# A two-layer hybrid decoder trunk on one core: two plain feed-forward blocks per layer in place of three, the second unit's head issued ahead of the first one's middle, and two token sums in one operation

## The chip, the cores and the metric

The kernel runs on one core of one Trainium2 chip. The metric is the device time of one execution in microseconds (us); the figure to compare is the median over several executions. Engines are called as the profile calls them: PE (TensorE, matmuls), PEld (its weight loads, which run beside its matmuls), DVE (VectorE), ACT (ScalarE), POOL (GpSimd) and SP (SyncE, which here only issues DMAs).

## The reference

Two decoder layers over 528 tokens (16 learned meta tokens and 512 real ones), model width 1024, in fp32. A layer is an attention part (a forgetting-attention head group and a retention head group behind one input projection, one output projection, residual) and a feed-forward part. Only the second is touched here:

```python
    hn = rmsnorm(h, ffn_norm_g)
    ff = jax.nn.silu(jnp.einsum('bld,df->blf', hn, w_gate)) * jnp.einsum('bld,df->blf', hn, w_up)
    return h + jnp.einsum('blf,fd->bld', ff, w_down)
```

w_gate and w_up are 1024 x 2816, w_down is 2816 x 1024. The meta tokens are dropped after the last norm, so the second layer's feed-forward part computes the 512 real tokens only.

## The kernel before, in words

**Layout.** Activations lie transposed: 128 features on the partitions, tokens along the free axis. The width of 1024 is `NK` = 8 tiles of 128, the 2816 hidden columns are `NF` = 22 blocks of 128, called f. Every product is done in three matmuls, because each fp32 operand is split into a high part (rounded to fp32r) and a low part (the rest): high x high, high x low, low x high. Each weight tile is split when it arrives, by one ACT copy (high part) and one subtraction (low part) on DVE, or on POOL in parts of the attention. In the feed-forward part POOL takes none of them.

**Plain blocks.** For f < `PLAIN` (3 before) gate and up are computed by `dense_steps`: 8 steps each, one per k, with six matmuls of 264 tokens in layer 0 and three of 512 tokens in layer 1. A job's step 1 and step 4 split the two halves of the next job's weights (`convert(j + 1, ...)`). `g_done` scales the gate sum and takes silu; `u_done` multiplies and splits the product into `ah` (ACT) and `al` (DVE), the input of the down projection (`acts[f]`).

**Units.** For f >= `PLAIN` gate and up of one f are computed together by a `Unit`: a scheme with seven half-size products in place of eight, on the two halves of the width (rows of the weights) and the two halves of the tokens. A half has w = 264 tokens in layer 0 and 256 in layer 1. One product is 4 k-steps of three matmuls of w tokens, so a unit has 7 x 12 = 84 matmuls. It needs sums of weights and sums of tokens:

- `head()`: two products, with the split gate weights (`make1`, job w1) and the plain tokens. It uses a bank x (pool `psa`) and a bank z (one half of a `psd` tile; the other half is y).
- `middle()`: three products, with job w2 (`make2`: two sums of gate and up weights, then a split) and the first half of job w3 (`make3`). It is the first to use the token sums `t`.
- `tail()`: two products, with the second half of w3 and job w4 (`make4`); its `done` adds the banks, takes silu, multiplies and splits into `ah`, `al`.

`need(j)` at the start of a product prepares job j and up to two unit or down jobs after it. `x_forms(k)`, k = 0..3, makes the token sums `t`: it scales two tiles of h into `S`, forms three differences there, and splits four pieces into `th` and `tl` (low part: one DVE operation of 4w elements a partition). `S` has two buffers, shared with the sums of weights.

**The order of the work.** PE executes the list `steps` as written (a manual schedule for PE alone). The other engines' instructions are ordered by a planner, which takes program order as the priority, takes what is ready in its own estimate of times, and lets blocks under `high_priority` go ahead. Each engine then executes its list strictly in that order. DMAs are issued from SP, in its own order. At the end of `ffn` further steps are put into the list: `squares` and `rstd` (the norm), the first gate's `g_done`, and the four `x_forms`, which are put 9 places apart, from place `NK + 4` on.

**Rounds.** `ROUNDS` groups the blocks f into (0, 3), (3, 7), (7, 11), (11, 15), (15, 19), (19, 22). While a round's units are computed, the down projection (`down_job`, `down`) of the round before is woven in: one pair of output tiles after each unit's middle and tail. In round 0 there is nothing to weave in. Jobs of units and down products (`add_job`) take turns between two rings of weight buffers, `whi`/`wlo` and `fwhi`/`fwlo`, of two buffers each; raw weights come into a ring of three buffers (`raw`) and one of two (`fraw`, w_up of the units). `psd` has two tiles of two banks, `psa` four banks.

The steps around the change, in the order in which PE meets them before: gate 0, up 0, gate 1, up 1, gate 2, up 2 (plain, `PLAIN` = 3), then unit 3: head, middle, down (first tile of the pair), tail, down (second tile), then unit 4, and so on.

Of the kernel before, what the change touches and what calls it, by code (L numbers as in the profile page):

```python
# [13 lines left out]
ALU = mybir.AluOpType  # L14

D = 1024
NK = D // 128
# [7 lines left out]
DFF = 2816  # L25
NF = DFF // 128
ROUNDS = ((0, 3), (3, 7), (7, 11), (11, 15), (15, 19), (19, 22))
PLAIN = 3
HB = NK // 2
EPS = 1e-6  # L30
NBLK = SEQ // 128
# [8 lines left out]
def hybrid_kernel(ctx, tc, x_t, w_in, w_fl, w_out, w_gate, w_up, w_down, vecs, b_fg, rope, decay, mask, ident, out_t):  # L40
    nc = tc.nc
# [95 lines left out]
    def vcol(c):  # L137
        return vec[:, c:c + 1]


    def split(hi, lo, src, pinned=False):
        pin(nc.scalar.copy(hi, src), pinned)
        pin(nc.vector.tensor_sub(lo, src, hi.bitcast(F32)), pinned)
# [53 lines left out]
    def dense_steps(src, parts, pool=False, banks=False, ahead=(1, 4), own=None, wait=None):  # L197

        j = len(jobs)
        jobs.append({"src": src, "pool": pool, "own": own})

        def chunk(k0, k, n, xs, cols, ps, done):
            def go():
                convert(j)
                if k == 0:
                    t = [psum_a() for _ in cols] if banks else psum()
                    ps.append(t)
                    ps.append(t if banks else [t[:, b] for b in range(2)])  # L210
                size = jobs[j]["w"][0][0]
                _, hi, lo = jobs[j]["w"][(k0 + k) // size]
                wk = (k0 + k) % size
                xh, xl = xs(k)
                for i, (w, x) in enumerate(((hi, xh), (hi, xl), (lo, xh))):
                    for b, (c0, c1) in enumerate(cols):
                        nc.tensor.matmul(ps[1][b][:, 0:c1 - c0], w[:, wk, :], x[:, c0:c1],  # L217
                                         start=(k == 0 and i == 0), stop=(k == n - 1 and i == 2))
                if k == n - 1:
                    done(ps[0]) if wait is None else wait.append(lambda: done(ps[0]))  # L220
                for half, at_step in enumerate(ahead):
                    if k0 + k == at_step:
                        convert(j + 1, 4 * half + 4)
            return go

        steps = []
        for k0, xs, n, cols, done in parts:
            ps = []
            steps += [chunk(k0, k, n, xs, cols, ps, done) for k in range(n)]
        return steps  # L230
# [42 lines left out]
    def fft(tag, dt=F32R, shape=(128, T), bufs=None):  # L273
        return phase["ffn"].tile(list(shape), dt, name=tag, tag=tag, bufs=bufs)
# [518 lines left out]
    def ffn(l, st, real, last):  # L793
        QC = REAL if real else FULL
        t0 = META if real else 0
        w = (T - t0) // 2
# [5 lines left out]
        def two(t):  # L802
            return t[:, t0:T].rearrange("p (a b) -> p a b", a=2)
# [4 lines left out]
        def g_done(f):  # L808
            def go(ps):
                sg = tt("sg")  # L810
                if isinstance(ps, list):
                    for v, (c0, c1) in zip(ps, QC):
                        nc.vector.scalar_tensor_tensor(sg[:, c0:c1], v[:, 0:c1 - c0], RSC, st["R"][:, c0:c1],
                                                       ALU.mult, ALU.mult)
                else:
                    nc.vector.scalar_tensor_tensor(sv(sg, real), pv(ps, real), RSC, sv(st["R"], real), ALU.mult, ALU.mult)
                silu(sv(sg, real))
                sgs[f] = sg
            return go

        def u_done(f):
            def go(ps):
                u = tt("tq")
                nc.vector.scalar_tensor_tensor(sv(u, real), pv(ps, real), RSC, sv(st["R"], real), ALU.mult, ALU.mult)
                nc.vector.tensor_mul(sv(u, real), sv(u, real), sv(sgs[f], real))
                fh, fl = act_tile(f)
                split(sv(fh, real), sv(fl, real), sv(u, real))
                acts[f] = (fh, fl)
            return go
# [4 lines left out]
        def x_forms(k):  # L834
            def go():
                if k == 0:
                    st["t"] = [[fft(f"t{p}{i}", shape=(128, 2, 4, w)) for p in "hl"] for i in range(2)]
                s = fft("S", F32, (128, 6, w), 2)
                a, b = ((h[k][:, c0:c1], h[HB + k][:, c0:c1]) for c0, c1 in HC)
                g0, g1 = vcol(V_FFN + l * NK + k), vcol(V_FFN + l * NK + HB + k)  # L840
                nc.scalar.activation(s[:, 0:2], two(h[k]), AF.Copy, scale=g0)
                nc.vector.tensor_sub(s[:, 2], s[:, 1], s[:, 0])
                for i in range(2):
                    nc.vector.scalar_tensor_tensor(s[:, 3 + i], b[1], g1, s[:, 1 + i], ALU.mult, ALU.subtract)
                nc.vector.scalar_tensor_tensor(s[:, 5], a[1], g1, s[:, 4], ALU.mult, ALU.subtract)
                th, tl = (t[:, k % 2] for t in st["t"][k // 2])
                split(th, tl, s[:, 2:6])
            return go
# [8 lines left out]
        def add_job(**job):  # L857
            job["ring"] = "f" if len(jobs) % 2 else ""
            jobs.append(job)
            return len(jobs) - 1  # L860
# [26 lines left out]
        class Unit:  # L887
            def __init__(self, f):
                self.f = f
                self.t = {}  # L890
                self.w1 = add_job(load=self.load, make=self.make1, n=NK)

            def rest(self):
# [91 lines left out]
        def down_job(p, f0, f1):  # L985

            n = f1 - f0
            t = {}

            def load():  # L990
                if t:
                    return
                t["r"] = wp.tile([128, NK, 128], F32, name="raw", tag="raw", bufs=3)
                for s in range(2):
                    nc.sync.dma_start(t["r"][:, s * n:s * n + n], w_down[l, 2 * p + s, :, f0:f1])

            return add_job(load=load, make=lambda hi, lo: splits(hi, lo, t["r"][:, 0:2 * n]), n=2 * n)
# [28 lines left out]
        steps = []  # L1026
        tails = []
        fills = []
        for r, (f0, f1) in enumerate(ROUNDS):
            for f in range(f0, f1):  # L1030
                if f < PLAIN:
                    steps += dense_steps(w_gate[l, f], [(0, xs, NK, QC, g_done(f) if f else held.append)], banks=f == 1)
                    steps += dense_steps(w_up[l, f], [(0, xs, NK, QC, u_done(f))])
                    continue
                u = Unit(f)
                steps += u.head()
                for v in tails:
                    v.last()
                    steps += v.tail()
                tails = []  # L1040
                u.rest()
                steps += u.middle()
                if fills:
                    p, g0, g1 = fills.pop(0)
                    j = down_job(p, g0, g1)
                    steps += down(j, 0, 2 * p, g0, g1, not real)
                    u.last()
                    steps += u.tail()
                    steps += down(j, 1, 2 * p + 1, g0, g1, False)
                else:  # L1050
                    tails = [u]
            for p, g0, g1 in fills:
                j = down_job(p, g0, g1)
                for s in range(2):
                    steps += down(j, s, 2 * p + s, g0, g1, False)
            fills = [(p, f0, f1) for p in range(NK // 2)]
# [157 lines left out]
                (after_0, after_1, after_2, after_3, after_4, after_5, after_6, after_7))]  # L1214
            steps += merge(rnd, places)
        for i in range(HB):
            steps.insert(NK + 4 + 9 * i, x_forms(i))
        steps.insert(NK + 4, lambda: g_done(0)(held[0]))
        steps.insert(NK + 4, lambda: rstd(st, QC))
        steps.insert(4, lambda: squares(st, QC, False, False))  # L1220
# [5 lines left out]
    def layer(l):  # L1226
# [79 lines left out]
        for g in range(2):  # L1306
# [15 lines left out]
                      ret_places(3, 52, 45.5, 47.5, 57.5, 55.5, 58.5, 60, 64.1, 63, 64.2))  # L1322
        plan += [op[3], op[7], op[11], op[15]] + op[16:]
        up = ffn(l, ff, real, real)
        plan += [lambda: enter("ffn"), start_ffn] + up
        return plan
# [78 lines left out]
```

## Time and profile before

| | before |
|---|---|
| time, median of 3 runs | 1272.0 us (1271.65 to 1273.03) |
| the profiled execution's own time | 1272.86 us |
| its span, first to last instruction | 1271.1 us |
| PE busy | 1256.1 us (99% of the span), 9271 matmuls |
| DVE busy | 996.9 us (78%), 1843 instructions |
| ACT busy | 687.2 us (54%) |
| POOL busy | 264.9 us (21%) |
| HBM traffic | 94 GB/s over the span |
| mean granted clock of PE | 0.997 |

Shares of busy time are averages over stages. The feed-forward part of layer 0 begins on PE at about 289.7 us (the first matmul that reads `xh`), that of layer 1 at about 913 us. In the rows of the profile a line shows the engine, the line of the kernel, the operation and "out<-in" by the tiles' names; L194, L217 and L191 are helpers that many steps share, and so are L868, L869 (the split of a unit's or down job's weights), L880 (a product of a unit), L142 and L143 (`split`). L1015 is a down projection's matmul, L914 to L927 the sums of weights, L841 to L845 the token sums. Matmul records overlap: a record of 264 tokens lasts some 0.28 us, while twelve of them follow one another in 1.45 us, so the time of PE is read from starts, or from the chain of work, and not from the sum of the records.

### The profile page before, as it was taken

The page shows a single profiled execution, that of the slowest core. Times are in us where ns is not written, and L with a number is a line of the kernel's source. Part 1 is how long each engine was busy: PE and PEld are TensorE (multiplying, and loading weights), DVE is VectorE, ACT ScalarE, POOL GpSimd, SP SyncE. Part 2 cuts the span into 40 slices and gives each one's busy share as a digit, 9 for nine tenths or more (in the row PEclk, how much of TensorE's full clock was granted, in tenths as well). Part 3 has the DMA queues.
Part 4 walks back from the last instruction along what each step waited for, and adds up shares of the span by engine and source line. Part 5 has one row for each costly group of instructions (what it writes and reads, how often), then busy time and mean ns, then how long its engine had stood idle before and what let it go on. Part 6 is the DMA issues. An engine that isn't in the chain of part 4 may idle for free.

```text
span 1271.1 us, 23615 instructions
## 1 busy us (share of the span) xinstructions
PE 1256.1 (99%) x9271; PEld 1197.9 (94%) x9271; DVE 996.9 (78%) x1843; ACT 687.2 (54%) x1246; POOL 264.9 (21%) x522
## 2 busy tenths in 40 slices
PE   9999999999999999999999999999999999999997
PEld 8999999999999999999999989999789999999996
DVE  7877856779988888887686877567899888888866
ACT  6666545676444444444455665457764444444444
POOL 3355546420000000000016546454100000000000
PEclk9999999999999999999999999999999999999998
DMA  6322222223333333332323132222233333333321
GB/s 217 93 68 84 78 90 76 73 71 113 108 96 100 100 100 101 100 100 84 101 76 116 61 101 85 76 92 68 100 95 121 100 100 100 101 100 100 103 80 67
DMA packets 45680, 120.57 MB, mean 95 GB/s; under 512 B 5360, under 2 KB 12272, under 8 KB 45568
## 3 DMA queue, kind: packets, MB, share of 16 engines
q1 hardware_dynamic: 45104, 118.74, 29.7%
q8 instruction: 73, 1.20, 0.4%
q10 hardware_dynamic: 464, 0.32, 0.1%
q14 instruction: 39, 0.32, 0.1%
HBM read 116.91 MB, written 2.13 MB: 94 GB/s over the span
## 4 chain that ended last, share of the span: by engine, by line
PE 92%; DVE 4%; ACT 2%; DMA 1%; issue 1%; ACTq 0%; DVEq 0%
PE psd L217 29%; PE psa L880 18%; PE psd L1015 14%; PE psd L880 13%; PE psa L217 5%; PE psa L1015 4%; PE psa L418 2%; PE psa L572 2%; PE psa L507 2%; PE psa L729 1%; PE psa L699 1%; PE psa L379 1%; DMA raw<-w_in 0%; ACT whi L191 0%; PE psa L290 0%
## 5 line engine op out<-in xcount | busy, mean ns | idle before, releaser
L194 POOL TENSOR_TENSOR wlo<-raw,whi 128x128 fp32r<-128x128 f32 x504 | 259.6, 549 | 289.1 <-ACT whi L191 289.0
L217 PE MATMUL psd<-xh,whi 128*128 128x264 f32 (+1 forms) x792 | 196.5, 316 | 0.7 <-ACT whi L191 0.7
L217 PE MATMUL psd<-xh,wlo 128*128 128x264 f32 (+1 forms) x792 | 187.2, 304 | 0.0
L217 PE MATMUL psd<-xl,whi 128*128 128x264 f32 (+1 forms) x792 | 186.7, 303 | 0.4 <-DVE xl L320 0.4
L217 PEld LDWEIGHTS psd<-xh,whi 128*128 128x128 f32 x792 | 128.9, 190 | 6.1 <-ACT whi L191 1.7
L217 PEld LDWEIGHTS psd<-xh,wlo 128*128 128x128 f32 x792 | 127.5, 189 | 6.2 <-DVE wlo L194 0.4
L217 PEld LDWEIGHTS psd<-xl,whi 128*128 128x128 f32 x792 | 128.0, 189 | 4.8 <-DVE xl L320 0.8
L191 ACT CAST whi<-raw 128x512 fp32r<-128x512 f32 (+1 forms) x168 | 98.3, 613 | 50.4 <-PE psd L217 37.5
L868 ACT CAST whi<-raw 128x1024 fp32r<-128x1024 f32 (+2 forms) x62 | 54.9, 885 | 51.3 <-PE psd L880 40.0
L868 ACT CAST fwhi<-raw 128x1024 fp32r<-128x1024 f32 (+2 forms) x62 | 55.6, 898 | 47.5 <-PE psd L880 40.0
L1115 POOL TENSOR_TENSOR th<-th,e 128x544 f32<-128x544 f32 x1 | 1.4, 1374 | 359.1 <-DVE e L1135 359.1
L85 POOL MEMSET kl<- 64x528 f32 x2 | 1.1, 534 | 345.4 <-PE psa L880 345.4
L869 DVE TENSOR_TENSOR wlo<-raw,whi 128x1024 fp32r<-128x1024 f32 (+2 forms) x62 | 62.9, 1015 | 12.8 <-ACT whi L868 12.7
L869 DVE TENSOR_TENSOR fwlo<-raw,fwhi 128x1024 fp32r<-128x1024 f32 (+2 forms) x62 | 64.0, 1032 | 10.3 <-ACT fwhi L868 10.1
L880 PE MATMUL psa<-th,whi 128*128 128x264 f32 (+1 forms) x232 | 65.4, 282 | 0.0
L880 PE MATMUL psa<-th,wlo 128*128 128x264 f32 (+1 forms) x232 | 65.4, 282 | 0.0
L880 PE MATMUL psa<-tl,whi 128*128 128x264 f32 (+1 forms) x232 | 65.3, 282 | 0.0
L880 PE MATMUL psa<-th,fwhi 128*128 128x264 f32 (+1 forms) x224 | 63.4, 283 | 0.0
L880 PE MATMUL psa<-tl,fwhi 128*128 128x264 f32 (+1 forms) x224 | 63.3, 283 | 0.0
L880 PE MATMUL psa<-th,fwlo 128*128 128x264 f32 (+1 forms) x224 | 63.2, 282 | 0.0
L527 ACT ACTIVATE probs<-probs,nmax 128x144 f32<-128x144 f32 (+1 forms) x64 | 36.9, 576 | 44.8 <-DVE nmax L514 31.9
L946 ACT COPY e<-psa 128x264 f32<-128x264 f32 (+1 forms) x114 | 42.8, 375 | 28.4 <-PE psa L880 24.1
(340 smaller groups left out, 4028.7 us busy)
## 6 DMA issues: line engine op xcount, KB each, us to landing
raw<-w_in SPq DMA_DIRECT2D x54, 512.0 KB, 3.5
raw<-w_gate SPq DMA_DIRECT2D x44, 512.0 KB, 3.8
fraw<-w_up SPq DMA_DIRECT2D x38, 512.0 KB, 3.5
raw<-w_down SPq DMA_DIRECT2D x64, 256.0 KB, 2.8
raw<-w_out SPq DMA_DIRECT2D x16, 512.0 KB, 3.4
raw<-w_down SPq DMA_DIRECT2D x32, 192.0 KB, 2.5
bc<-cdr SPq DMA_DIRECT2D x16, 264.0 KB, 3.4
raw<-w_up SPq DMA_DIRECT2D x6, 512.0 KB, 3.5
```

What stands on the lines that cost most here:

```text
L191: pin(nc.scalar.copy(hi, job["raw"][:, c0:c1]), pinned)
L194: pin(sub(lo[:, i:i + step], job["raw"][:, c0 + i:c0 + i + step], hi[:, i:i + step].bitcast(F32)), pinned)
L217: nc.tensor.matmul(ps[1][b][:, 0:c1 - c0], w[:, wk, :], x[:, c0:c1], start=(k == 0 and i == 0), stop=(k == n - 1 and i == 2))
L418: nc.tensor.transpose(ps[:, 128 * j:128 * j + 128], src[:, o:o + 128], idt)
L507: nc.tensor.matmul(sc[0:nq, 0:c1 - c0], st["q"][s][:, q0:q0 + nq], kk[:, c0:c1], start=(i == 0), stop=(i == 1))
L527: nc.scalar.activation(pr, pr, AF.Exp, bias=nmax[0:nq], scale=-1.0, accum_out=rsum)
L572: nc.tensor.matmul(po[:, c0:SEQ], v[:, j, :], pp[:, j, META + c0:T], start=(j == 0 and i == 0), stop=(j == 4 and i == 1))
L868: nc.scalar.copy(hi, src)
L869: nc.vector.tensor_sub(lo, src, hi.bitcast(F32))
L880: nc.tensor.matmul(bank()[:, 0:b.shape[-1]], a[:, o + k, :], b, start=(fresh and k == 0 and i == 0), stop=(k == n - 1 and i == 2), skip_gr ...
L946: nc.scalar.copy(self.t["e"][:, i], self.t["x"][:, 0:w])
L1015: nc.tensor.matmul(v[:, 0:c1 - c0], a[:, s * n + k, :], b[:, c0:c1], start=(k == 0 and i == 0), stop=(k == n - 1 and i == 2))
```

## The change

`PLAIN` goes from 3 to 2, so f = 2 becomes a unit in both layers; the rounds stay. For the first unit (f == `PLAIN`) the next unit, f = 3, is created at once, and its head is put behind the first one's head, ahead of that one's middle. When f = 3 comes, its head is skipped. Since no down projection is ready in round 0, unit 2's tail comes after its middle with nothing between. PE's new order is: gate 0, up 0, gate 1, up 1, head 2, head 3, middle 2, tail 2, middle 3, down, tail 3, down, head 4, and so on. In `x_forms` the two differences s[3] and s[4] are written by one operation on twice the elements, its first operand repeated. The four `x_forms` are put 6 places apart and not 9.

```diff
-PLAIN = 3
+PLAIN = 2
...
-                for i in range(2):
-                    nc.vector.scalar_tensor_tensor(s[:, 3 + i], b[1], g1, s[:, 1 + i], ALU.mult, ALU.subtract)
+                nc.vector.scalar_tensor_tensor(s[:, 3:5], b[1].unsqueeze(1).broadcast_to([128, 2, w]), g1, s[:, 1:3],
+                                               ALU.mult, ALU.subtract)
...
                 self.t = {}
+                self.begun = False
                 self.w1 = add_job(load=self.load, make=self.make1, n=NK)
...
         fills = []
+        ahead = []
         for r, (f0, f1) in enumerate(ROUNDS):
             for f in range(f0, f1):
                 if f < PLAIN:
...
                     continue
-                u = Unit(f)
-                steps += u.head()
+                u = ahead.pop() if ahead else Unit(f)
+                if not u.begun:
+                    steps += u.head()
+                if f == PLAIN:
+                    ahead.append(Unit(f + 1))
+                    ahead[0].begun = True
+                    steps += ahead[0].head()
                 for v in tails:
                     v.last()
                     steps += v.tail()
...
         for i in range(HB):
-            steps.insert(NK + 4 + 9 * i, x_forms(i))
+            steps.insert(NK + 4 + 6 * i, x_forms(i))
```

## The prediction

> **What bounds the kernel now.** I read the page's first part, then the waits of PE, then stretches around the start of the feed-forward part with the busy time of each engine, then the chain of work there, then DVE's instructions in order of time.
>
> ```profile
> PE 1256.1 (99%) x9271; PEld 1197.9 (94%) x9271; DVE 996.9 (78%) x1843; ACT 687.2 (54%) x1246; POOL 264.9 (21%) x522
> ...
> PE psa L1257 <- DVE wide L61: 1.6, 1, 1.6
> ```
>
> PE is the bound, busy 99% of the span; its longest single wait in the whole kernel is 1.6 us, before the first work. So matmul time that goes is time won, unless PE then waits for another engine. Which one that would be is in two stretches, the first in layer 0, the second in layer 1 (columns: PE, PEld, DVE, ACT, POOL busy, granted clock, DMA share, GB/s).
>
> ```profile
> 305.00:320.00 15.00, 15.00 (x126) 15.00 (x126) 15.00 (x28) 8.44 (x12) 0.00 (x0) 1.00 0.28 79
> ...
> 935.00:950.00 15.00, 15.00 (x75) 12.55 (x74) 15.00 (x23) 9.31 (x13) 0.00 (x0) 1.00 0.21 62
> ```
>
> In the plain blocks DVE is as full as PE: 15.00 of 15 us, in both layers, while ACT has a third or more free. The average of 78% hides this. PE doesn't wait here only because DVE is a few us ahead of it. The change shortens PE's work in this very place, and the question is what becomes of that lead.
>
> **What PE saves.** The chain of work gives PE's pace (start, us, what, count of matmuls).
>
> ```profile
> 308.01 17.36 PE psd L217 x144
> ...
> 328.26 1.45 PE psa L880 x12
> ...
> 409.95 1.48 PE psa L880 x12
> ...
> 412.89 2.92 PE psd L1015 x24
> 415.82 1.45 PE psa L880 x12
> ...
> 423.06 1.95 PE psa L1015 x16
> ...
> 931.47 16.66 PE psd L217 x72
> ...
> 950.96 1.42 PE psa L880 x12
> ...
> 1045.37 1.42 PE psa L880 x12
> ...
> 1048.20 2.77 PE psd L1015 x12
> 1050.97 1.42 PE psa L880 x12
> ...
> 1058.07 2.08 PE psd L1015 x9
> ```
>
> Layer 0: three plain jobs (up 1, gate 2, up 2) take 17.36 us, so gate 2 with up 2 takes 11.57. A unit is the stretch from 409.95 to 412.89 and that from 415.82 to 423.06, with down matmuls between: 2.94 + 7.24 = 10.18. The block f = 2 saves 1.39 us. Layer 1: 16.66 x 2/3 = 11.11, against (1048.20 - 1045.37) + (1058.07 - 1050.97) = 9.93, so 1.18 us. Together 2.57 us, which is 0.2% of the time and about what a measurement of this kernel can tell from no change. The gain has this ceiling; a loss has none so near.
>
> **What is late next: DVE, layer 0.** These rows are in DVE's order (start, duration; the next start shows what an instruction really costs, about 0.1 less than its duration).
>
> ```profile
> 315.98 0.70 DVE L825 TENSOR_TENSOR tq<-tq,sg 128x528 f32<-128x528 f32 x1
> 316.60 0.49 DVE L845 SCALAR_TENSOR_TENSOR S<-h,vec,S 128x264 f32<-128x264 f32 x1
> 317.00 0.69 DVE L194 TENSOR_TENSOR wlo<-raw,whi 128x512 fp32r<-128x512 f32 x1
> 317.60 0.70 DVE L143 TENSOR_TENSOR al<-tq,ah 128x528 fp32r<-128x528 f32 x1
> 318.22 0.69 DVE L914 TENSOR_TENSOR S<-fraw 128x512 f32<-128x512 f32 x1
> 318.82 1.25 DVE L143 TENSOR_TENSOR tl<-S,th 128x1056 fp32r<-128x1056 f32 x1
> 319.99 0.70 DVE L816 SCALAR_TENSOR_TENSOR sg<-psd,R 128x528 f32<-128x528 f32 x1
> 320.61 1.22 DVE L869 TENSOR_TENSOR wlo<-raw,whi 128x1024 fp32r<-128x1024 f32 x1
> 321.74 0.69 DVE L915 TENSOR_TENSOR S<-S,raw 128x512 f32<-128x512 f32 x1
> 322.34 0.69 DVE L921 TENSOR_TENSOR fraw<-raw,fraw 128x512 f32<-128x512 f32 x1
> 322.95 0.68 DVE L927 TENSOR_TENSOR raw<-raw,S 128x512 f32<-128x512 f32 x1
> 323.55 1.22 DVE L869 TENSOR_TENSOR fwlo<-S,fwhi 128x1024 fp32r<-128x1024 f32 x1
> 324.69 0.95 DVE L869 TENSOR_TENSOR fwlo<-raw,fwhi 128x768 fp32r<-128x768 f32 x1
> ```
>
> The first unit's middle starts at 328.26; its third matmul, 0.24 us on, is the first to need the low part `fwlo` of `make2`, which DVE finishes at 324.7. The lead is 3.8 us. At 319.99 DVE has finished the last token sum (`tl`), both plain blocks' ends, the splits of gate 2 and up 2, and one sum of `make2` (L914).
>
> Now the new order. Up 1 ends where gate 2 began, at 308.01 + 5.79 = 313.80. Head 2 and head 3 follow, 2.89 each (325.37 to 328.26 for one), so head 3 starts at 316.69 and middle 2 at 319.58. DVE's list up to there, from 319.99:
> - out go four splits of gate 2 and up 2 (317.00 to 317.60, 0.60 each): 2.40; L914 is counted below: 0.60; the pair operations, next paragraph: 0.52. That gives 316.47.
> - in come `make1` of units 2 and 3, each 1.13 (320.61 to 321.74): 318.73. Head 3's third matmul needs the second at 316.93, so PE waits 1.8 us.
> - then L914, L915 (1.20) and the low part of `make2` (1.14): 321.07, and 322.28 if L921 and L927 (1.21) go ahead of it as they do now, while ACT makes the high part. Middle 2, put off to 321.38, needs it at 321.62: 0 to 0.65 more.
>
> So 1.8 to 2.45 us in layer 0, if the planner keeps program order. If it lets the last two operations of `u_done(1)` (L825 and L143 `al`, 0.62 each) come later, which nothing near needs, 0.6 to 1.2.
>
> **The pair operation.** One operation of 528 elements in place of two of 264, at eight places:
>
> ```profile
> L320 DVE SCALAR_TENSOR_TENSOR xl<-h,vec,xh 128x528 fp32r<-128x528 f32 x8 | 5.9, 764 | 0.0
> ...
> L844 DVE SCALAR_TENSOR_TENSOR S<-h,vec,S 128x264 f32<-128x264 f32 x8 | 3.6, 492 | 0.0
> ```
>
> 2 x 0.492 - 0.764 = 0.22 less the 0.09 by which successive records overlap: 0.13 us each, 0.52 a layer, if the repeated operand costs nothing. No row shows one; at twice L320's pace the pair would lose 0.5 each instead, which I hold unlikely, as `xl` reads the same number of elements. It is on DVE alone and counts through the lead above.
>
> **Layer 1, the same way.**
>
> ```profile
> 942.12 0.69 DVE L914 TENSOR_TENSOR S<-fraw 128x512 f32<-128x512 f32 x1
> 942.72 1.23 DVE L143 TENSOR_TENSOR tl<-S,th 128x1024 fp32r<-128x1024 f32 x1
> 943.87 0.69 DVE L816 SCALAR_TENSOR_TENSOR sg<-psd,R 128x512 f32<-128x512 f32 x1
> ```
>
> The plain jobs end at 948.13 and would end 11.11 earlier, at 937.02; head 3 would start at 939.85, middle 2 at 942.68 (a head is 950.96 - 948.13 = 2.83). DVE: 943.87 - 2.40 - 0.60 - 0.52 + 2.26 = 942.61 for head 3's low part, needed at 940.08: 2.5 us late. `make2` then ends at 944.95 to 946.16, needed at 945.44: 0 to 0.7 more. So 2.5 to 3.2, or 1.3 to 2.0 with the deferral. DVE's lead is smaller here, which is why it costs more.
>
> **Down waits for unit 2.** Round 0's down projection reads `acts[2]` in its third step. Before, block 2 was plain and long done. Now unit 2's tail ends, then comes middle 3 (4.35 us) and two thirds of 2.2 us of down, so `al` is needed 6.1 us after the tail's end (layer 1: 5.8). What a unit's end takes is in these rows: the chain, then DVE, in layer 0 and in layer 1.
>
> ```profile
> 336.27 1.47 PE psd L880 x12
> ...
> 344.51 0.71 DVE L143 TENSOR_TENSOR al<-tq,ah 128x528 fp32r<-128x528 f32 x1
> ...
> 960.10 2.06 PE psd L1015 x9
> ...
> 967.67 0.69 DVE L143 TENSOR_TENSOR al<-tq,ah 128x512 fp32r<-128x512 f32 x1 [0.69 <-ACT ah L142]
> ```
>
> From 337.74 to 345.2 is 7.5 us, from 960.10 to 968.4 is 8.3: taken so, 1.4 and 2.5 us late. But much of that is other work of DVE in between (the down weights and sums into h), which isn't there when unit 2 ends; without it there is no wait. I take 0.4 in each layer, nearer the lower end, and keep 0 to 3.9 for both.
>
> **What costs nothing.** Behind middle 2's start DVE has `make3` and `make4` of unit 2 and `make2` of unit 3, 1.74 + 1.20 + 2.34 = 5.3 us, and PE five products, 7.25 us, before it needs the last: no further wait. Head 3's weights come by one more of these:
>
> ```profile
> raw<-w_gate SPq DMA_DIRECT2D x44, 512.0 KB, 3.8
> ```
>
> They land 3.8 us after issue; before, two more `raw` tiles were loaded for gate 2 and up 2, now one for unit 2, so SP's queue gets shorter in this place and no ring slot is asked for earlier. `fraw` for both units has its two buffers, loaded at the stage's start. The two open units hold both `psd` tiles and two of four `psa` banks; the next to ask for a `psd` tile comes after unit 2's end. If the first read of up 1's sum were late, head 3's z product would wait for it; it has 4.3 us. ACT gets one and a half more copies of 1024 elements and three of a bank in a layer, at DVE's prices 1.5 x 1.22 + 3 x 0.49 = 3.3 us, and has 5.7 of 15 free. POOL is idle here.
>
> **Sum.** -2.57 + 1.8 + 2.5 + 0.8 = +2.5 us. I take the low ends of the program-order bounds, because fillers would run where DVE now has ACT's gaps. From the profiled execution's own 1272.86 that is 1275.4; it stands 0.86 above the median, so 1274.5 for the median.
>
> **Rivals.**
> - The full gain: the planner puts both `make1` ahead of the token sums and block ends, and heads 2 and 3 (5.8 us) cover the rest. For it: a head needs no token sum, and ACT has room. Against it: even with the best order DVE's list up to middle 2 is 0.6 us too long, 1.3 in layer 1. It needs 2 us less of DVE work than I count in each layer. 1272.0 - 2.57 = 1269.4.
> - Deferral: `u_done(1)` late, no wait for `acts[2]`: -2.57 + (0.6 to 1.2) + (1.3 to 2.0) = -0.7 to +0.6, so 1271.3 to 1272.6: no change.
> - Down waits fully: 3.9 in place of 0.8 gives 1277.6. It decides once DVE is more than 0.8 us behind at unit 2's end.
> - The clock falls. The granted clock is 1.00 in all stretches shown, after waits of 1.6 us at most; layer 1's wait may come to 3.2. If PE then ran at half speed for the next two groups of twelve (1.42 each), that is 2.8 us more: 1277.3. [...]
>
> **How the numbers follow.** My case (1273.2 to 1276.2, about half of it beyond 0.2%) 0.40; deferral 0.25; full gain 0.19; down waits 0.12; clock 0.04. Faster by over 0.2% (2.5 us) needs the full gain and a little luck: 0.15. Slower: 0.23 of my case, the down wait and the clock: 0.39. The rest, 0.46, is within. The range goes from the full gain's 1269.4 to 1278.0, just beyond the full down wait. My case's own range is 1273.2 to 1276.2.
>
> **What would show it.** Right: PE's waits name L880 on DVE L869 (or ACT L868) at head 3 or middle 2, 1 to 3 us in each layer and more in layer 1; DVE is full from the stage's start to there; a unit's 84 matmuls take 10.2 and 9.9 us. A wait of L1015 on `ah` or `al` in the first down product would be the second step. Wrong: no wait of PE at these places; `make1`'s L869 ahead of the last `tl`; or the loss lying in another stage, where the planner, given another program, has ordered DVE anew.

## Result, and the profile after

The changed kernel takes 1288.4 us in the median (1287.5 to 1289.2) against 1272.3 for the kernel before: ratio 1.0126, 95% interval 1.0114 to 1.0138, or 16 us slower. The forecast was 1274.5 with a range up to 1278.0: right in the direction, and too small by a factor of six.

The page after, first line of part 1, and the part of the waits of PE that is new (engine, tile, line, releaser: us in total, times, longest). Before, none of these rows existed.

```profile
PE 1261.0 (98%) x9295; PEld 1202.8 (93%) x9295; DVE 1006.8 (78%) x1849; ACT 693.3 (54%) x1252; POOL 264.9 (21%) x522
...
PE psa L880 <- ACT whi L868: 3.3, 2, 1.8
PE psa L880 <- DVE wlo L869: 2.1, 3, 0.8
...
PE psd L1016 <- ACT ah L142: 1.2, 1, 1.2
PE psa L1016 <- ACT ah L142: 1.1, 1, 1.1
PE psa L880 <- DVE fwlo L869: 0.9, 1, 0.9
PE psa L880 <- ACT e L947: 0.9, 2, 0.5
...
PE psd L1016 <- DVE al L143: 0.7, 1, 0.7
...
PE psa L1016 <- DVE al L143: 0.6, 1, 0.6
```

The idle times add up to 10.8 us, all within the 30 us behind the plain blocks of each layer. They understate the loss a little: the modelled end of a matmul lies some 0.16 us behind its slot (a record lasts 0.28 us, the next starts 0.12 after it), so I count a wait as the gap between two starts less the usual pace. Here is the first middle in layer 0, PE in order of time (start, duration; idle time and releaser in brackets).

```profile
319.83 0.28 PE L880 MATMUL psd<-xh,fwlo 128*128 128x264 f32 x1
321.69 0.39 PE L880 MATMUL psa<-th,whi 128*128 128x264 f32 x1 [1.58 <-ACT whi L868]
321.92 0.28 PE L880 MATMUL psa<-tl,whi 128*128 128x264 f32 x1
322.95 0.39 PE L880 MATMUL psa<-th,wlo 128*128 128x264 f32 x1 [0.75 <-DVE wlo L869]
323.18 0.28 PE L880 MATMUL psa<-th,whi 128*128 128x264 f32 x1
...
324.59 0.42 PE L880 MATMUL psd<-th,whi 128*128 128x264 f32 x1
324.81 0.42 PE L880 MATMUL psd<-tl,whi 128*128 128x264 f32 x1
...
327.39 0.28 PE L880 MATMUL psa<-tl,fwhi 128*128 128x264 f32 x1
327.51 0.28 PE L880 MATMUL psa<-th,fwlo 128*128 128x264 f32 x1
```

Three things are to be seen. From 319.83 to 322.95 PE stands still for 1.74 and 0.91 us, first for the high part of unit 2's sums of weights, then for its low part. The first matmul behind a wait takes 0.23 us to the next start (321.69 to 321.92), where the usual pace is 0.12. And from 323.9 to 327.2 all matmuls start every 0.22 us. The granted clock of such stretches confirms this last one (stretch, its length, PE busy, granted clock, DMA share, GB/s):

```profile
318.80:322.20 3.40, 1.81 (x13) 1.00 0.00 0
322.20:325.60 3.40, 2.65 (x15) 0.75 0.11 13
325.60:329.00 3.40, 3.29 (x21) 0.75 0.73 295
329.00:332.40 3.40, 3.04 (x24) 1.00 0.41 141
...
339.20:342.60 3.40, 2.44 (x11) 0.76 0.02 5
342.60:346.00 3.40, 3.40 (x23) 0.74 0.00 0
...
954.60:958.00 3.40, 2.64 (x13) 0.61 0.15 17
958.00:961.40 3.40, 3.28 (x25) 0.89 0.79 266
```

Two neighbouring rows of 3.4 us at 0.75 each, or at 0.61 and 0.89, are half the clock for 3.4 us. It happens three times: twice in layer 0, once in layer 1 (granted clock 0.50 from 323.88 to 327.29, from 340.95 to 344.36 and from 955.35 to 958.76, 3.41 us each). Here is what DVE does meanwhile, and the copy on ACT between two of its operations; in this execution the stage begins some 0.4 us earlier than in the profile of before.

```profile
312.97 1.22 DVE L869 TENSOR_TENSOR wlo<-raw,whi 128x1024 fp32r<-128x1024 f32 x1
314.11 0.49 DVE L845 SCALAR_TENSOR_TENSOR S<-h,vec,S 128x264 f32<-128x264 f32 x1
314.51 0.70 DVE L824 SCALAR_TENSOR_TENSOR tq<-psd,R 128x528 f32<-128x528 f32 x1
315.13 1.22 DVE L869 TENSOR_TENSOR fwlo<-raw,fwhi 128x1024 fp32r<-128x1024 f32 x1
316.26 1.25 DVE L143 TENSOR_TENSOR tl<-S,th 128x1056 fp32r<-128x1056 f32 x1
317.43 0.70 DVE L825 TENSOR_TENSOR tq<-tq,sg 128x528 f32<-128x528 f32 x1
318.05 1.29 DVE L915 TENSOR_TENSOR S<-fraw 128x512 f32<-128x512 f32 x2
319.25 0.70 DVE L143 TENSOR_TENSOR al<-tq,ah 128x528 fp32r<-128x528 f32 x1
319.87 0.69 DVE L916 TENSOR_TENSOR S<-S,raw 128x512 f32<-128x512 f32 x1
320.47 0.69 DVE L922 TENSOR_TENSOR fraw<-raw,fraw 128x512 f32<-128x512 f32 x1
321.07 0.69 DVE L928 TENSOR_TENSOR raw<-raw,S 128x512 f32<-128x512 f32 x1
321.68 1.22 DVE L869 TENSOR_TENSOR wlo<-S,whi 128x1024 fp32r<-128x1024 f32 x1
```
```profile
320.59 1.04 ACT L868 CAST whi<-S 128x1024 fp32r<-128x1024 f32 x1 [1.52 <-DVE S L916]
```

DVE has no gap. It ends the low part of `make2` at 322.9; the prediction's account, moved by those 0.4 us, gives 320.7 to 321.9, and PE, had it never waited, would have read it at 319.4. That is 3.5 us late, about what PE's three waits of this layer add up to (0.75 at head 2, 1.74, 0.91).

The difference put together from PE's starts, layer 0 and layer 1:

| us | predicted | layer 0 | layer 1 | both |
|---|---|---|---|---|
| matmuls saved | -2.57 | -1.39 | -1.18 | -2.57 |
| waits at the heads and the first middle | 4.3 | 0.75 + 1.74 + 0.91 | 1.10 + 1.91 + 0.92 | 7.3 |
| tail 2 for the copy out of bank x | 0 | 0.63 | 0.62 | 1.25 |
| first down product for `acts[2]` | 0.8 | 1.26 + 0.92 | 1.40 + 0.93 | 4.5 |
| matmuls at half clock | 0 | 1.50 + 1.65 | 1.47 | 4.6 |
| the slower first matmul behind each wait | 0 | 0.45 | 0.43 | 0.9 |
| sum | 2.5 | | | 16.0 |

The spans of the two profiles differ by 1286.8 - 1271.1 = 15.7.

### The profile page after: what moved, and what is told of

Same layout as the page of the kernel before. It is cut to its first block, busy times and chain, and to the rows that moved or that the text cites. A ratio compares the mean times of both kernels' runs of the same rounds, so it can differ in the third digit from the quotient of the medians.

```text
span 1286.8 us, 23676 instructions
## 1 busy us (share of the span) xinstructions
PE 1261.0 (98%) x9295; PEld 1202.8 (93%) x9295; DVE 1006.8 (78%) x1849; ACT 693.3 (54%) x1252; POOL 264.9 (21%) x522
## 3 DMA queue, kind: packets, MB, share of 16 engines
HBM read 116.91 MB, written 2.13 MB: 93 GB/s over the span
## 4 chain that ended last, share of the span: by engine, by line
PE 88%; DVE 7%; ACT 3%; issue 1%; DMA 1%; DVEq 0%; ACTq 0%
PE psd L217 26%; PE psa L880 19%; PE psd L1016 14%; PE psd L880 13%; PE psa L1016 4%; PE psa L217 4%; PE psa L418 2%; PE psa L572 2%; PE psa L507 1%; PE psa L729 1%; PE psa L699 1%; PE psa L379 1%; DVE tl L143 0%; ACT whi L191 0%; DVE fwlo L869 0%
## 5 line engine op out<-in xcount | busy, mean ns | idle before, releaser
L217 PE MATMUL psd<-xh,whi 128*128 128x264 f32 (+1 forms) x744 | 183.6, 315 | 0.5 <-ACT whi L191 0.5
L217 PE MATMUL psd<-xh,wlo 128*128 128x264 f32 (+1 forms) x744 | 174.5, 303 | 0.0
L217 PE MATMUL psd<-xl,whi 128*128 128x264 f32 (+1 forms) x744 | 173.9, 302 | 0.4 <-DVE xl L320 0.4
L217 PEld LDWEIGHTS psd<-xh,whi 128*128 128x128 f32 x744 | 121.0, 191 | 4.8 <-ACT whi L191 1.2
L217 PEld LDWEIGHTS psd<-xh,wlo 128*128 128x128 f32 x744 | 119.6, 189 | 5.6 <-DVE wlo L194 0.4
L217 PEld LDWEIGHTS psd<-xl,whi 128*128 128x128 f32 x744 | 120.1, 189 | 4.1 <-DVE xl L320 0.8
L191 ACT CAST whi<-raw 128x512 fp32r<-128x512 f32 (+1 forms) x160 | 93.7, 613 | 48.5 <-PE psd L217 37.1
L868 ACT CAST fwhi<-raw 128x1024 fp32r<-128x1024 f32 (+2 forms) x64 | 57.8, 903 | 49.3 <-PE psd L880 38.2
L868 ACT CAST whi<-raw 128x1024 fp32r<-128x1024 f32 (+2 forms) x64 | 56.1, 877 | 51.2 <-PE psd L880 41.1
L869 DVE TENSOR_TENSOR fwlo<-raw,fwhi 128x1024 fp32r<-128x1024 f32 (+2 forms) x64 | 66.4, 1038 | 11.1 <-ACT fwhi L868 11.0
L869 DVE TENSOR_TENSOR wlo<-raw,whi 128x1024 fp32r<-128x1024 f32 (+2 forms) x64 | 64.3, 1005 | 12.4 <-ACT whi L868 12.3
L880 PE MATMUL psa<-th,fwhi 128*128 128x264 f32 (+1 forms) x240 | 68.2, 284 | 0.9 <-ACT e L947 0.9
L880 PE MATMUL psa<-tl,fwhi 128*128 128x264 f32 (+1 forms) x240 | 68.0, 283 | 0.0
L880 PE MATMUL psa<-th,fwlo 128*128 128x264 f32 (+1 forms) x240 | 67.9, 283 | 0.0
L947 ACT COPY e<-psa 128x264 f32<-128x264 f32 (+1 forms) x120 | 45.2, 376 | 36.1 <-PE psa L880 32.1
```

The costliest lines, as they stand in the source:

```text
L191: pin(nc.scalar.copy(hi, job["raw"][:, c0:c1]), pinned)
L880: nc.tensor.matmul(bank()[:, 0:b.shape[-1]], a[:, o + k, :], b, start=(fresh and k == 0 and i == 0), stop=(k == n - 1 and i == 2), skip_gr ...
L947: nc.scalar.copy(self.t["e"][:, i], self.t["x"][:, 0:w])
```

## Experiments

The theory after the result: DVE has more to do ahead of the first middle than PE's two heads cover, the rest follows from the new order (a tail behind its middle, a result needed at once), and the waits bring PE's clock down. Each ratio below is to the kernel before as measured beside that run (medians from 1271.6 to 1272.6 us), so a difference of under 1 us between two of these kernels says nothing. Rivals: the open second unit harms; the new places of the token sums harm; the round trip DVE, ACT, DVE sets the waits and not DVE's load.

**Which part of the change.** First the head ahead taken back:

```diff
-                if f == PLAIN:
-                    ahead.append(Unit(f + 1))
-                    ahead[0].begun = True
-                    steps += ahead[0].head()
```

> The changed kernel (1288.4 us) without the second unit's head ahead of the first one's middle. Theory (DVE has too much to do before the first middle): the cover of 2.9 us goes and only one split of 1.1 us goes with it, so PE waits about 1.8 us longer in each layer: 1291 to 1294. Rival (two open units are what harms, by holding both double banks): the waits go, and it comes near 1280.

1289.3 us, 1.0132 (1.0117 to 1.0148): no better without it, and less worse than expected. The wait at the first middle grows by 0.6 us in layer 0 and by 2.0 in layer 1. The open unit by itself isn't what harms.

Then the spacing of 9 in place of 6:

> The changed kernel with the token sums 9 places apart, as before. Theory: DVE's total ahead of the first middle is the same, so within 1.5 us of 1288.4. Rival (the earlier token sums push the splits of units 2 and 3 late): 4 us or more less, 1284 or lower.

1281.5 us, 1.0069 (1.0052 to 1.0086): 7 us better, a miss for the theory and the number that the rival gave. The trace shows where it comes from: the waits counted by starts fall only from 13.1 to 11.2 us, while no stretch at half clock is left, which is worth 4.4. So the places of the token sums do harm, but mostly through the clock. At the first middle up to 2.65 and 2.83 us of waiting fell within 3.4 us; now it is 1.7 and 2.4, and the low part of the last token sum is what PE waits for:

```profile
PE psa L880 <- ACT e L947: 2.1, 2, 1.1
PE psa L880 <- DVE tl L143: 1.8, 2, 0.9
...
PE psd L1016 <- ACT ah L142: 1.4, 1, 1.4
...
PE psa L880 <- ACT th L142: 0.8, 2, 0.4
```

Then the kernel before with the pair operation and the spacing of 6 alone:

> The kernel before, with only the pair operation and the spacing of 6. Theory: no wait of PE stood there, so within 1.3 us of 1272.3. Rival (the new order of DVE, or a slow repeated operand, is the loss): 1276 or more.

1272.4 us, 0.9998 (0.9989 to 1.0008). These two are neutral where PE isn't waiting.

**The clock.** Ahead of the first middle stand matmuls that nothing reads:

```diff
                     steps += ahead[0].head()
+                    steps.append(lambda: fill(7))
...
+        def fill(count):
+            idle = psum_a()
+            for _ in range(count):
+                nc.tensor.matmul(idle, ones, st["x"][0][0][:, META:T], start=True, stop=True)
```

> The changed kernel with seven matmuls of 512 tokens into an unused bank ahead of the first unit's middle, about 1.6 us of PE time where it now stands idle 1.7 to 1.9 us; nothing reads them. [...]

1285.4 us, 1.0108 (1.0091 to 1.0125): 3 us less (2.3 by the ratios) for more work, about what the half clock behind the two first middles costs by the table (1.50 and 1.47). PE now goes through the same place like this:

```profile
319.16 1.80 PE L1030 MATMUL psa<-xh,ones 128*128 128x512 f32 x7
320.92 0.39 PE L880 MATMUL psa<-th,whi 128*128 128x264 f32 x1
321.15 0.28 PE L880 MATMUL psa<-tl,whi 128*128 128x264 f32 x1
322.18 0.39 PE L880 MATMUL psa<-th,wlo 128*128 128x264 f32 x1 [0.75 <-DVE wlo L869]
322.41 0.29 PE L880 MATMUL psa<-th,whi 128*128 128x264 f32 x1
322.53 0.29 PE L880 MATMUL psa<-tl,whi 128*128 128x264 f32 x1
```

The low part still comes late, by the same 0.75, and behind it the pace is 0.12 from the second matmul on; the granted clock is 1.00 from 318.8 to 329.0, where it was 0.75 in the rows from 322.2 on. So the slow matmuls were the clock's doing, and PE's idleness brought it on. The two slow stretches of layer 0 are gone; in layer 1 one is left, now behind the down product's wait.

**DVE's load.** The low parts of block 1's weights on POOL:

```diff
-                    steps += dense_steps(w_gate[l, f], [(0, xs, NK, QC, g_done(f) if f else held.append)], banks=f == 1)
-                    steps += dense_steps(w_up[l, f], [(0, xs, NK, QC, u_done(f))])
+                    steps += dense_steps(w_gate[l, f], [(0, xs, NK, QC, g_done(f) if f else held.append)], f == 1, banks=f == 1)
+                    steps += dense_steps(w_up[l, f], [(0, xs, NK, QC, u_done(f))], f == 1)
```

> The changed kernel with the low parts of the weights of gate 1 and up 1 made on POOL, idle here, and not on DVE: 2.4 us of DVE's work less in each layer, nothing else. Theory: the waits at the heads and the first middle (4.0 us in layer 0, 4.3 in layer 1) shrink by 2.4 each, and the stretches at half clock behind them (1.6 each) go: 1280 to 1281; the waits of the first down product for unit 2 stay. Rival (the waits are the latency from DVE over ACT to DVE, and not DVE's load): less than 2 us better, 1286 or more.

1287.9 us, 1.0123 (1.0108 to 1.0138): nothing won, as the rival said. But the trace shows that DVE got little of the relief that the experiment was for. The same DVE operations from 295.5 to 308.4 us, first with POOL at work (x count, busy, mean ns), then in the changed kernel with POOL idle:

```profile
L143 DVE TENSOR_TENSOR tl<-S,th 128x1056 fp32r<-128x1056 f32 x2 | 3.0, 1516 | 0.8 <-ACT th L142 0.8
L843 DVE SCALAR_TENSOR_TENSOR S<-h,vec,S 128x528 f32<-128x528 f32 x3 | 2.8, 966 | 0.0
```
```profile
L143 DVE TENSOR_TENSOR tl<-S,th 128x1056 fp32r<-128x1056 f32 x2 | 2.5, 1257 | 0.2 <-ACT th L142 0.2
L843 DVE SCALAR_TENSOR_TENSOR S<-h,vec,S 128x528 f32<-128x528 f32 x3 | 2.3, 776 | 0.0
```

Five groups of DVE's operations, the two shown among them, last 0.19 to 0.26 us longer each while POOL subtracts; over this window that is 2.0 of the 2.4 us taken off. The waits at the heads and the first middle did fall, from 7.3 to 5.0 us, but PE gained 0.6 of waiting in the plain blocks of each layer, and the wait for bank x grew from 1.25 to 2.4. So the run decides nothing between theory and rival. Next the work was left out instead of moved: block 1's weights get no low part, and the high part is multiplied in its place.

```diff
+            if job["same"]:
+                t = wp.tile([128, NK, 128], F32R, name="whi", tag="whi")
...
+            job["split"] = c1
+            if job["same"]:
+                continue
```

> The changed kernel without the subtraction that makes the low parts of gate 1's and up 1's weights: the high part is multiplied in its place, so PE does the same matmuls and DVE 2.4 us less ahead of the first middle, with no work on POOL. Theory (DVE's load): the waits at the heads and the first middle (3.4 us in layer 0, 3.6 in layer 1) shrink to 1 to 1.3 and the half clock behind them goes: about 1288.4 - 4.7 - 3.2 = 1280.5. Rival (the order of DVE's work and its round trips with ACT): less than 3 us better.

1283.3 us, 1.0086 (1.0071 to 1.0101): 5 us better, between the two expectations. The waits at heads and first middle go from 7.3 to 3.5 us, so DVE's load counts; but the wait for bank x, no longer behind the others, grows from 1.25 to 2.4, and one slow stretch stays.

Next, order at the same load: block 1's last operations behind the third unit's head (product and split of `u_done` go into a list, `put_off`, that a step there works off):

```diff
+                    steps.append(lambda: put_off.pop()())
```

> The changed kernel with the last operations of block 1 (its product and its split, 1.9 us of DVE, whose result the first down product needs much later) put in program order behind the third unit's head and the preparation of the first middle. Theory (DVE works off program order, and what stands ahead of the first middle's sums without need is what PE waits for): the waits of 2.65 us at the first middle shrink by 1.2 to 1.9 in each layer, one or two of three stretches at half clock go: 1281 to 1285. Rival (the round trip from DVE over ACT to DVE alone sets the wait): above 1287.

1282.7 us, 1.0080 (1.0065 to 1.0095), within the expectation. The first middle waits 1.57 and 1.62 us in place of 2.65 and 2.83, and no stretch at half clock is left, so more than half of the gain is the clock's.

**The down product.** For the first unit of round 1 the tail goes ahead of the first down product:

```diff
+                    if f == PLAIN + 1:
+                        u.last()
+                        steps += u.tail()
                     steps += down(j, 0, 2 * p, g0, g1, not real)
-                    u.last()
-                    steps += u.tail()
+                    if f > PLAIN + 1:
+                        u.last()
+                        steps += u.tail()
```

> The changed kernel with the first down product put behind the third unit's tail, so that unit 2's result has 2.9 us more. Theory: the waits on its high and low part (2.3 us in layer 0, 1.9 in layer 1) go, and the half clock behind them in layer 0 (1.6): 1282 to 1283. Rival (DVE is behind altogether and the wait only moves): less than 2 us better.

1286.0 us, 1.0110 (1.0095 to 1.0125): less than half of what was expected. Of the waits of 4.5 us only 0.6 for `al` is left in each layer, but a tail now stands directly behind unit 3's middle too and waits 0.63 and 0.62 for bank x, and in layer 1 the slow matmuls behind the first middle's wait are spread over 5.9 us (953.62 to 959.52, starts 0.21 to 0.22 us apart) and not 3.3 (955.56 to 958.87 in the changed kernel).

The same with the spacing of 9:

> The changed kernel with the token sums 9 places apart and the first down product behind the third unit's tail. Theory: of 1281.5 with the spacing alone, the waits for unit 2's result (1.9 and 2.2 us) go: 1277 to 1278, still behind the kernel before, since the waits at the first middle and for the shared bank (4 us over both layers) stand against 2.6 us saved. Rival (the wait only moves): 1280 or more.

1278.5 us, 1.0053 (1.0038 to 1.0068), 0.5 above what the theory gave. With the deferral instead:

> The changed kernel with block 1's last operations put off and the first down product behind the third unit's tail. Theory: of 1282.7 with the first alone, the waits for unit 2's result go (4.5 us over both layers), and a wait for the shared bank of 0.6 comes in its place in each layer: 1279 to 1280. Rival (the waits only move): above 1281.

1279.1 us, 1.0053 (1.0038 to 1.0068), within the expectation: 9.3 us less than the changed kernel, against 8.2 for the two gains alone.

**Is bank x a wait by itself?** From the last kernel, the third unit's head is cut in two, and its second product put between middle 2 and tail 2:

> The same, with the second product of the third unit's head put between unit 2's middle and tail, where PE waits for the copy out of bank x (1.5 and 0.9 us). Theory (DVE and ACT set the pace of the whole stretch, so cover taken from the first middle is missed there): that wait goes, the one at the first middle grows by about as much: within 1.5 us of the run before, 1279 to 1281. Rival (the bank is a wait by itself): 2 us or more better.

1283.0 us, 1.0088 (1.0071 to 1.0105): worse, by more than the theory allowed. The wait for bank x behind middle 2 is gone (1.55 and 0.90 us), the one at the first middle has grown by about as much or more (the high part's from 0.65 to 2.11 and from 0.71 to 2.13), and this lump brings a slow stretch in each layer, which the two smaller waits did not. Cover is only moved about here.

**Other rounds**, (0, 2), (2, 6) and so on, so that down products of round 0 stand behind unit 2's middle and tail, the first of them in single banks (spacing of 9):

> The changed kernel with the token sums 9 places apart and rounds of (0, 2), (2, 6), (6, 10), (10, 14), (14, 18), (18, 22), so that unit 2 too has down products behind its middle and its tail; the one behind its middle takes single banks in both layers. Theory: the waits for the shared bank and for unit 2's result (7.3 us over both layers with the spacing alone) have something to cover them and go, those at the first middle stay (1.7 and 2.4), against 2.6 saved: 1273 to 1275. Rival (DVE is behind for the whole stretch, and each wait moves to the next place): 1277 or more.

1288.0 us, 1.0126 (1.0109 to 1.0142), a miss. The waits it was for are gone, but others come: the second down product waits 1.6 and 1.5 us until a double bank is read out (L957; the two open units held both), and at each layer's end the last unit's result is now needed at once (2.1 us at 631 us, 3.1 at 1252).

```profile
PE psd L1016 <- DVE sg L957: 3.2, 2, 1.6
PE psa L880 <- ACT ah L142: 3.1, 1, 3.1
PE psd L1016 <- ACT ah L142: 2.1, 1, 2.1
```

With the deferral as well:

> The kernel with the other rounds and the spacing of 9, and with block 1's last operations put behind the third unit's head. Theory: 1.2 to 1.9 us less waiting at the first middle in each layer than with the rounds alone: 1270 to 1273, level with the kernel before or just ahead of it. Rival: no better than the rounds alone.

1291.0 us, 1.0145 (1.0130 to 1.0160), a miss again: the first middle waits 3.2 and 3.5 us for `th` and `tl`, and half clock follows in both layers (starts 0.21 to 0.22 us apart).

**How much relief it takes.** From the kernel with deferral and later down product, the subtractions for block 1's weights left out, then those of all plain blocks:

> The first of these four without the subtractions for the low parts of gate 1's and up 1's weights (the high part is multiplied in their place): 2.4 us of DVE less in each layer. Theory (DVE's load): the waits at the first middle (1.6 and 1.6) go: 1275 to 1277. Rival (round trips): above 1278.

> The same without the subtractions for all plain blocks' weights: 4.8 us of DVE less in each layer. Theory: with enough taken off DVE only the waits for bank x are left (1 to 3 us) against 2.6 saved: 1270.5 to 1273, level with the kernel before. Rival (something other than DVE's load holds the two heads and the first middle): above 1275.

1277.7 us, 1.0040 (1.0025 to 1.0055), a little short of the expectation (0.92 and 0.91 us of waiting are left at the first middle), and 1272.7 us, 1.0006 (0.9996 to 1.0015), within it. In the last one PE no longer waits at the heads or at the first middle. What is new against the kernel before:

```profile
PE psa L892 <- ACT e L959: 2.1, 4, 0.7
...
PE psd L1028 <- DVE al L143: 0.5, 1, 0.5
```

By starts these are 2.9 us over both layers beyond the wait that the kernel before had, against 2.57 saved: level. So with enough of DVE's work gone, the waits at the heads and the first middle go, and the slow stretches behind them: DVE's load holds these places, and ACT's copy between two of its operations doesn't by itself. These two runs also have the deferral and the later down product; whether that much relief would do without them wasn't run. Bank x is a cost of the order by itself, 0.62 to 0.90 us each time a tail follows its middle directly, with DVE's load gone. No kernel that computes the whole was faster than the one before.

## Why the prediction was right and wrong

The direction, the engine and the place were right, and the sign named came: PE waits for L869 and L868 at a head and at the first middle, though 3.4 and 3.9 us a layer where I had named 1 to 3. What failed is the size of the DVE term and three terms that I put at nothing or near it.

- **What PE saves** agrees in size: f4 with 2.9 us of waits is level with the kernel before, which leaves about 2.8 us for the saving, give or take 1.2.
- **DVE is late next**: the size was 7.3 us, above the 4.3 of the sum and above my upper ends too, 5.65. The step that failed is that head 3 would take the wait and the first middle need at most 0.7 more. In layer 0 head 3 had none (in layer 1 1.10): DVE made its low part (315.13) ahead of the last token sum and block 1's last operations, and these then stood ahead of `make2`. There the chain is longer than I counted. The first middle reads the high part first, which ACT copies from the sum of L916 in 1.04 us; only then can DVE begin the low part. L922 and L928 merely filled that time on DVE, so my low end, 321.07, which has no copy in it, could not have been reached. I took the low ends "because fillers would run where DVE now has ACT's gaps", and DVE had none. Besides, one of unit 3's two sums went ahead (the second L915 of the pair at 318.05, 0.6 us), which is in none of my bounds. These 0.6 a layer are most of what is above the upper ends; the rest stays open. Head 2 had 0.75 in layer 0: its low part came at 312.97 only, behind a token sum's.
- **"No further wait" behind the first middle** failed. I counted DVE's work against PE's products there and left out a dependency: tail 2 writes bank x, which ACT must first copy out (L947), and in every other round a down product of 2.2 us stands between. 1.25 us.
- **Down waits for unit 2**: 4.5 us, beyond the upper end of 3.9. I took 0.8 on the ground that the other work of DVE "isn't there when unit 2 ends". It was: unit 3's sums and splits and the down weights stood between these two, the first and the last of DVE's rows for unit 2's end in layer 0:

```profile
332.80 0.70 DVE L957 TENSOR_TENSOR sg<-psd,e 128x528 f32<-128x528 f32 x1
...
339.91 0.70 DVE L143 TENSOR_TENSOR al<-tq,ah 128x528 fp32r<-128x528 f32 x1
```

  From the tail's end, 332.4, to the end of `al`, 340.6, it is 8.2 us where I had room for 6.1, and 8.1 in layer 1 where I had 5.8; the 7.5 and 8.3 us of the kernel before were the rows to take.
- **The clock** was a rival at 0.04, resting on a wait of up to 3.2 us in layer 1; no row of before shows half speed, and its price of 2.8 us was my estimate. It cost 4.6 us. The step that failed was to look for one long wait: there are three stretches with a granted clock of 0.50 for 3.41 us, which cost 1.47 to 1.65 us each, and no single wait reached 2 us. In the 3.4 us ahead of each PE had been idle for 2.1 to 2.6 us, in pieces.
- **The pair operation** costs what the prediction said: 0.68 us from start to start (L843 twice in 1.36 us, 308.05 to 309.41), so the repeated operand costs nothing here; alone with the spacing it changes nothing.

## What to carry to other kernels

Where PE is 99% busy, look for the stretch where another engine is just as full, and take that engine's lead in us as the budget of any change that shortens PE's work there; here 3.8 us of lead met 8.7 us less of PE time ahead of the first middle (11.57 for gate 2 and up 2 gone, 2.89 for a second head come). When an order is changed, ask of each pair of steps that become neighbours what had stood between them: a bank that must be copied out, a result that has a long way to its reader. And price waits with what they do to the clock: here several short ones close together cost 4.6 us beyond their sum. Where work on one engine needs a copy by another in between, count that copy in the chain, not only the busy time.

## What the runs showed of the hardware

- In the stretches behind the plain blocks PE ran at half clock in fifteen places of eight of these kernels: in the changed kernel by the granted clock (0.50 for 3.41 us, three times), in the others by starts 0.21 to 0.22 us apart in place of 0.12. In the 3.4 us ahead of each PE had stood idle for at least 1.7 us, mostly in pieces; yet 2.2 and 2.5 us of 3.4 with the spacing of 9 were followed by no slow stretch. In twelve places the slow matmuls are spread over 3.2 to 3.7 us, in three over 5.9 to 6.8 (layer 1 of b1, a1 and r3). With matmuls that nothing reads in the idle time ahead of the first middle the granted clock stayed at 1.00 there, and the time fell by 2 to 3 us.
- The clock isn't the same in every execution of a kernel: of d1's four executions one shows a mean clock of 0.998 and took 1280.9 us, the others 0.995 and 1283.2 to 1284.2. What decides between 1.7 us of idle time with a fall and 2.5 without one was not shown.
- While POOL subtracted, five groups of DVE's operations were 0.19 to 0.26 us longer (1516 against 1257 ns, 966 against 776 in the rows shown); L842, the difference of 264 elements, was not (429 against 438). So of the 2.4 us moved from DVE to POOL 2.0 were lost again.
